# Alternating the two column halves of TensorE's array in a two-layer hybrid trunk

## The chip, the cores and the metric

The kernel runs on one core of a Trainium2 chip. The metric is device time in microseconds: the median of repeated executions, which agree with each other to a few hundredths of a per cent. Beside it stands one execution recorded by the hardware profiler, and all rows below come from that one.

The engines are called by their names in the profile: PE is TensorE's matmul side, PEld its weight loads, DVE is VectorE, ACT is ScalarE, POOL is GpSimd, SP the engine that issues the weight DMAs.

## The reference, cut to what matters

Two layers, 512 tokens, 1024 channels. Three mixers run side by side on one normalised input `h`, each is gated, projected and merged, and the result goes through an output projection onto the residual. Two of the mixers hold the products that the change touches:

```
# stick-breaking attention, 8 heads of 64 channels, 128-query blocks
z = q[:, start:end] @ k[:, :end].T * scale
w = where(causal, exp(log_sigmoid(z) + after), 0)      # after: sums of log_sigmoid(-z)
out = w @ v[:, :end]                                   # 64 channels per head

# state space, 32 groups of 16 channels, 64 complex states per group
h = associative_scan(a_bar, u @ b_bar)
y = h_re @ c_re - h_im @ c_im + d * u
```

Everything is in float32. The big projections are made of float32 values split into a high and a low part (three products each); the products of this change take plain float32 operands.

## The kernel before

**Slots.** A layer is a list of main products (`mm`, 24 or 12 passes over the array each), written out by hand in `ORDER_TEXT`. One main product is a slot. The mixers are Python generators beside it: a generator is spawned for a slot, issues some instructions, and says how many slots later it goes on. Its TensorE instructions stand before the main product of the slot (`advance`). The order on every engine is therefore fixed when the program is built; nothing is chosen at run time.

**Weights.** SP loads each weight tile (`raw`), ACT copies it into a high part (`wh`, L316), DVE subtracts to get the low part (`wl`, through the helper at L197). Four units are made ahead.

**Line numbers.** Every product and many vector operations go through counting helpers, so that their line is L197. They are told apart by the tile that they write.

**The attention output** (`sb_pair`, L1010, product `sbo`, L1097). A generator treats two heads. Each head has 64 channels, so its output has 64 rows: the first head's output goes to partitions 0 to 63 of one PSUM tile, the second head's to 64 to 127. Per head there are four products, one for each block of 128 keys, over 512, 384, 256 and 128 query columns, summed in PSUM. `v` is the stationary operand, [128 keys, 64 channels], so that a product occupies 64 of the array's 128 columns. There are four such generators in a layer, so eight `sbo` stretches in all. The transposed weights `wt0`, `wt13`, `wt2` come from `turned` (L1067), written by ACT and DVE a slot earlier.

**The state space output** (`ssm`, L870, product `py`, L917). A generator treats eight groups, in pairs of products: inputs times `mt` (the part within a chunk of tokens), then states `H` times `ca`, summed in PSUM. The stationary operand is [128, 64], the moving one 128 columns. Groups 0 to 3 go to partitions 0 to 63, groups 4 to 7 to 64 to 127. There are four such generators in a layer, so eight `py` stretches.

**Passes.** The trace shows each of these float32 products as two passes, each a weight load and a matmul record: 128 records stand for 64 products.

**The products of `within`** (tile `pk`, L773) are not touched. Each writes 32 partitions, so that it occupies a quarter of the array's columns, and the eight of them are issued to the four quarters in turn.

Of the kernel before, what the change touches and what calls it, by code (L numbers as in the profile page):

```python
# [27 lines left out]
# the products of a layer, in order: name, or name:first-last unit  # L28
# [6 lines left out]
# the schedule  # L35
K = dict(
    # tiles of the pools, and how far weights are loaded and split ahead
    nw=12, w=4, raw=4, b=48,
    # starts and distances of the parts beside the main products, in slots
    sb0=0, sb_gap=4, ssm0=6, ssm_gap=3, ret0=9, ret_gap=3, x0=-3, x1=2, ret_pre=4, lead=9,  # L40
    # shares of a slot that GpSimd and VectorE give to the tables
    g=0.9, v=0.7,
    # slots between the steps of a part
# [6 lines left out]
# columns of the combined input projection  # L50
# [8 lines left out]
# the products of a layer, in order: 512 columns by blocks of tokens ...  # L59
BY_TOKEN = "sq sk sv cu rq rk rv0 rv1 out0 out1".split()  # L60
# ... or one unit of weights at a time (eight products of 128 columns, or four of twice that)
# [7 lines left out]
# small parameters of a layer: columns of one [128, NPAR] array  # L69
# [16 lines left out]
def _tm(w, c0):  # L86
    """512 columns, four units of two 128-row blocks."""
    a = w[:, c0 : c0 + 512].reshape(4, 2, P, 512)
    return a.transpose(0, 2, 1, 3).reshape(4, P, 1024)


def _cm(w, c0):
    """128 columns, eight 128-row blocks: one unit."""
    return w[:, c0 : c0 + 128].reshape(8, P, 128).transpose(1, 0, 2).reshape(1, P, 1024)


def _cm2(w, c0):
    """256 columns of a matrix of 512 rows: one unit."""
    return w[:, c0 : c0 + 256].reshape(4, P, 2, 128).transpose(1, 2, 0, 3).reshape(1, P, 1024)


def _layout(i):
# [27 lines left out]
    for l in range(L):  # L130
        def put(n, a):
            c, s = PAR[n]
            par[l, :, c : c + s] = a

        def pg(a):  # [32, 64, ...] -> [(2 p), 32 ...]
            a = np.swapaxes(a, 0, 1).reshape(64, -1)
            return np.concatenate([a, a])

        put("rqg", i["ret_q_norm"][l][None])
        put("rkg", i["ret_k_norm"][l][None])  # L140
        put("sqg", np.tile(i["sb_q_norm"][l], 2)[:, None])
        put("skg", np.tile(i["sb_k_norm"][l], 2)[:, None])
        put("rog", i["ret_out_norm"][l].reshape(8, P).T)
        put("bglu", i["ssm_b_glu"][l].reshape(4, P).T)
        put("are", pg(i["ssm_a_re"][l]))
        put("aim", pg(i["ssm_a_im"][l]))
        put("ldt", pg(np.repeat(i["ssm_log_dt"][l][:, None], 64, 1)))
        # [(group of four, 2, channel), (quarter, half)]
        d = i["ssm_d"][l].reshape(4, 2, 4, 1, 16)
        put("dsk", np.broadcast_to(d, (4, 2, 4, 2, 16)).transpose(2, 3, 4, 0, 1).reshape(P, 8))  # L150
        for n in range(2):
            bc[l, n] = pg(i[("ssm_b_re", "ssm_b_im")[n]][l])
            bc[l, 2 + n] = pg(np.swapaxes(i[("ssm_c_re", "ssm_c_im")[n]][l], 1, 2))
# [4 lines left out]
def _constants():  # L158
    """Of shapes alone: rotary angles, retention's decays, masks."""
# [27 lines left out]
def trunk(ctx: ExitStack, tc, x_in, w_in, par_in, bc_in, ng_in, cst_in, rope_in, out):  # L187
# [3 lines left out]
    def counted(f, engine, each):  # L191
        """f, with its time in microseconds added to the load of its engine in this slot."""
# [63 lines left out]
    def spawn(gen, slot, front=False):  # L256
        """Start `gen` in a slot, one per main product. It yields how many slots later to go on: its products come
        before the slot's main one, 0 is for what follows them in the same slot."""
# [10 lines left out]
    def then(gen):  # L269
        """What follows a main product, in the next slot."""  # L270
        spawn(gen, now[0] + 1, True)

    def rsqrt_mean(out_, ssum, n, eps, cols):
        """out = (ssum / n + eps) ** -0.5 on Pool."""
# [18 lines left out]
    class Weights:  # L293
# [4 lines left out]
        def room(self, n):  # L298
            """Is there room for n more tiles: two of a unit in use, one of a loaded one?"""
# [36 lines left out]
    def three(ps, a, b, first, last):  # L336
        """ps += a.T @ b in float32's accuracy; a, b: (high, low) parts."""
# [13 lines left out]
    def token_major(lhs, evac):  # L351
        """512 columns of h @ w: one main product for each block of tokens."""
# [27 lines left out]
    def channel_piece(evac, rhs, nk, n, pair=None):  # L380
        """128 columns; with nk = 4 a unit holds two such."""
# [96 lines left out]
    # Its coefficients, of both layers at once  # L478
# [10 lines left out]
    def ks(n):  # L489
        """A temporary of the tables."""  # L490
# [13 lines left out]
    # powers e = 0 .. 8 of the discrete pole a: (Re, -Im) a^e above and (Im, Re) a^e below  # L504
    Y = [kc(n, NS * 9).rearrange("p (g e) -> p g e", e=9) for n in ("y_re", "y_im")]
    # unit phasors u = exp(8 i theta), conjugate above: fine[b] = u^(b+1), coarse[a] = u^(8 a)
# [3 lines left out]
    def cmul(o_re, o_im, a_re, a_im, b_re, b_im, tmp, eng=None):  # L510
        """o = a * b; tmp: three tiles' views like o."""
# [9 lines left out]
    def tables():  # L521
# [20 lines left out]
        # th: the angle in [-pi, pi]; sine and cosine from those of its half  # L542
# [17 lines left out]
        # q1: the discrete pole's conjugate  # L560
# [3 lines left out]
        # coef = (a_bar - 1) / a  # L564
# [35 lines left out]
        def times(tab, lo, m, to, a):  # L600
            """tab[to + i] = tab[lo + i] * a for i < m"""
# [26 lines left out]
        for m in (1, 2, 4):  # L628
            # coarse[m + 1 ...] = coarse[1 ...] * coarse[m]
# [10 lines left out]
    def cmul_steps(o_re, o_im, a_re, a_im, b_re, b_im, tmp, e=GT, every=1):  # L640
        """The same, an operation at a time."""
# [10 lines left out]
    class Coef:  # L652
        """One layer's matrices, emitted piece by piece."""
# [12 lines left out]
        def emit(self):  # L666
# [16 lines left out]
            # c's output is a real part: c below with the other sign  # L683
# [6 lines left out]
        def quarter(self, q, bb, cc):  # L690
# [19 lines left out]
            # states' input: a^(7-j) b  # L710
# [20 lines left out]
            # rotations exp(8 i theta (c + 1)), conjugate above  # L731
# [13 lines left out]
            # states' output: Re above, -Im below of c a^e, e = 0 .. 8  # L745
# [13 lines left out]
            # b for the products with it, twice  # L759
# [10 lines left out]
            # inputs within a chunk of eight tokens: Re(c a^(j-i) b), and the skip on the diagonal; two tokens' rows  # L770
            # at a time, the odd ones' a token later
# [36 lines left out]
    def layer(l, last, base):  # L808
# [23 lines left out]
        def qk_evac(dst, gain, l1, l2):  # L832
            """Normalised, transposed: [2 heads' channels, pair of heads, token]."""
# [36 lines left out]
        def ssm(q):  # L870
            win, ca, mt, T = coef.q[q]
            p0 = G * l + 8 * q
            # inputs of the groups, (token in chunk, channel) on partitions
# [14 lines left out]
            # rotate back, scan with the real decay, rotate on: the part by the sine comes from the other half  # L888
# [21 lines left out]
            # states after each chunk, moved on by one  # L910
# [5 lines left out]
            # the first four groups' chunks on the upper partitions, the others' on the lower  # L916
            py = psm("py")  # L917
            for n in range(8):
                sl = slice(n * 64, n * 64 + 64)
                o = py[64 * (n // 4) : 64 * (n // 4) + 64, n % 4 * P : n % 4 * P + P]  # L920
                k = 2 * (n % 2) + n // 4
                MM(o, ut[:, sl], mt[n % 4 // 2][:, k * P : k * P + P], start=True, stop=False)
                MM(o, H[:, sl], ca[:, n, 1:9, :].rearrange("p a b -> p (a b)"), start=False, stop=True)
# [15 lines left out]
            # gelu (tanh form): y * sigmoid(2 sqrt(2 / pi) (y + 0.044715 y^3))  # L939
# [68 lines left out]
        sbo = [None] * 4  # L1008

        def sb_pair(pr):  # L1010
# [3 lines left out]
            # by head: q's high part twice, and k's high and low parts, on the two halves of the partitions  # L1014
# [23 lines left out]
            def weights_of(ps, segs, sg):  # L1038
                """Stick-breaking weights, in sg; the running products of what is kept go from the right."""
# [58 lines left out]
            for h in range(2):  # L1098
                r = half[h]
                c = slice(128 * pr + 64 * h, 128 * pr + 64 * h + 64)  # L1100
                MM(po[r, :], sv[0][:, c], wt0[h], start=True, stop=False)
                MM(po[r, 128:512], sv[1][:, c], wt13[h][:, 0:384], start=False, stop=False)
                MM(po[r, 256:512], sv[2][:, c], wt2[:, 256 * h : 256 * h + 256], start=False, stop=False)
                MM(po[r, 384:512], sv[3][:, c], wt13[h][:, 384:512], start=False, stop=True)
# [15 lines left out]
        def load_rope(gain, rope):  # L1120
            # the norm's gain goes into the rotation's cosines and sines
# [48 lines left out]
        def ret_chunk(n):  # L1170
# [9 lines left out]
            def halves(c):  # L1180
                """By half: the parts of v, and the two parts of the others in one tile."""
# [131 lines left out]
        def quarters():  # L1313
            """The state space's quarters, as their matrices come."""
# [73 lines left out]
```

## Time and profile before

| what | value |
|---|---|
| median of 3 runs | 1353.73 us (1353.4 to 1353.94) |
| span of the profiled execution, first to last instruction | 1352.2 us |
| PE busy | 1321.8 us (98%) |
| PEld busy | 1069.4 us (79%) |
| DVE busy | 853.7 us (63%) |
| ACT, POOL busy | 537.0 us, 375.5 us |
| mean granted TensorE clock | 0.994 |

The profiled execution's own span is 1.5 us shorter than the median of the runs, which also holds what lies around the span. "Busy" of PE is the time in which at least one pass is somewhere in the array, and a pass stays in the records for longer than the distance to the next one, so that the share says nothing about how well the array's columns are filled. How long a stretch of products takes is read from the start of its first pass to the start of the first pass behind it.

In a timeline row, the first number is the start, the second the time that the merged group covers, "x16" the number of records merged, "128*64" the stationary operand's rows and columns, "128x512" the moving operand. In brackets stands the idle time of the engine before it and what ended it.

### The profile page before, as it was taken

The numbers are of one execution on the slowest core, as the hardware profiler recorded it, in microseconds if no ns is written. First come the engines' busy times: TensorE is split into PE (matmuls) and PEld (weight loads), VectorE is DVE, ScalarE is ACT, GpSimd is POOL, SyncE is SP. The second block draws the span as 40 slices with busy tenths as digits, with TensorE's granted clock in tenths as the row PEclk, the third lists the DMA queues.
The fourth block names the chain that finished last, engine by engine and source line by source line (L and its number), as shares of the span: only waits on it lengthen the run. The fifth ranks groups of instructions, "written<-read, shape, count | busy, mean of one in ns | idle before, by whom it ended". The sixth has DMA issues, their size and how long they took to land. (4 is left out here: it accounts for less than half of the span.)

```text
span 1352.2 us, 16611 instructions
## 1 busy us (share of the span) xinstructions
PE 1321.8 (98%) x6360; PEld 1069.4 (79%) x6360; DVE 853.7 (63%) x1189; ACT 537.0 (40%) x919; POOL 375.5 (28%) x436
## 2 busy tenths in 40 slices
PE   7989989999999999999999999899999999999998
PEld 5867768788887888888888777688888878888887
DVE  5996676776687338556365566778646845485542
ACT  5435433534434434332233444343443434333321
POOL 3230035737534013000052000576374420220000
PEclk9989989999999999999999999999999999999999
DMA  5332120222232221224533222112232224223332
GB/s 216 99 120 63 63 63 23 87 78 95 79 94 78 92 80 63 81 91 141 166 119 119 78 63 63 47 63 79 78 112 76 63 63 125 63 78 91 97 126 77
DMA packets 37375, 120.05 MB, mean 89 GB/s; under 512 B 4144, under 2 KB 4528, under 8 KB 37296
## 3 DMA queue, kind: packets, MB, share of 16 engines
q1 hardware_dynamic: 29664, 105.40, 24.6%
q10 hardware_dynamic: 7632, 13.59, 3.0%
q8 instruction: 50, 0.82, 0.2%
q14 instruction: 29, 0.24, 0.1%
HBM read 114.78 MB, written 4.19 MB: 88 GB/s over the span
## 5 line engine op out<-in xcount | busy, mean ns | idle before, releaser
L197 DVE TENSOR_TENSOR wl<-raw,wh 128x1024 fp32r<-128x1024 f32 x196 | 250.3, 1286 | 127.5 <-ACT wh L316 125.4
L197 PE MATMUL mm<-hh,wh 128*128 128x512 f32 x640 | 257.7, 403 | 0.0
L197 PE MATMUL mm<-hh,wl 128*128 128x512 f32 x640 | 253.1, 395 | 2.3 <-DVE wl L197 2.3
L197 PE MATMUL mm<-hl,wh 128*128 128x512 f32 x640 | 251.0, 392 | 0.0
L316 ACT ACTIVATE wh<-raw 128x1024 fp32r<-128x1024 f32 x196 | 206.0, 1057 | 85.7 <-PE mm L197 41.3
L197 PE MATMUL mm<-wh,hh 128*128 128x512 f32 x512 | 209.9, 410 | 0.8 <-ACT hh L419 0.8
L197 PE MATMUL mm<-wl,hh 128*128 128x512 f32 x512 | 204.9, 400 | 4.1 <-DVE wl L197 4.0
L197 PE MATMUL mm<-wh,hl 128*128 128x512 f32 x512 | 204.0, 399 | 0.0
L197 PEld LDWEIGHTS mm<-hh,wl 128*128 128x128 f32 x640 | 120.9, 189 | 30.6 <-DVE wl L197 3.6
L197 PEld LDWEIGHTS mm<-hh,wh 128*128 128x128 f32 x640 | 121.3, 190 | 24.8 <-issue 1.8
L197 PEld LDWEIGHTS mm<-hl,wh 128*128 128x128 f32 x640 | 121.2, 189 | 24.5
L197 PEld LDWEIGHTS mm<-wl,hh 128*128 128x128 f32 x512 | 104.9, 205 | 25.3 <-DVE wl L197 6.8
L197 PEld LDWEIGHTS mm<-wh,hh 128*128 128x128 f32 x512 | 104.7, 205 | 20.9 <-ACT hh L419 1.2
L197 PEld LDWEIGHTS mm<-wh,hl 128*128 128x128 f32 x512 | 104.6, 204 | 20.7 <-DVE hl L197 0.3
L1046 DVE TENSOR_TENSOR_SCAN kp<-kp,zero 128x511 f32<-128x511 f32 (+1 forms) x64 | 60.4, 964 | 36.8 <-ACT kp L1042 36.4
L987 ACT ACTIVATE gate<-mm 128x512 f32<-128x512 f32 x48 | 28.6, 595 | 123.4 <-PE mm L197 123.4
L197 POOL TENSOR_SCALAR ms<-ss 128x8 f32<-128x8 f32 (+3 forms) x56 | 19.1, 341 | 186.5 <-DVE ss L822 101.8
L1024 POOL CAST qd<-qd 64x512 fp32r<-64x512 f32 x16 | 15.8, 987 | 194.6 <-ACT qd L1020 179.6
L197 POOL TENSOR_TENSOR rs<-ms,mhalf 128x8 f32<-128x8 f32 (+3 forms) x56 | 64.7, 1155 | 4.7
L820 ACT ACTIVATE sq<-mm 128x512 f32<-128x512 f32 x32 | 19.0, 592 | 88.5 <-PE mm L197 88.5
L197 PE MATMUL mm<-wl,mgh 128*128 128x512 f32 x128 | 50.1, 391 | 0.2
L197 PE MATMUL mm<-wh,mgh 128*128 128x512 f32 x128 | 49.9, 390 | 0.0
(254 smaller groups left out, 2312.9 us busy)
## 6 DMA issues: line engine op xcount, KB each, us to landing
raw<-in_w SPq DMA_DIRECT2D x196, 512.0 KB, 3.5
x<-in_x SPq DMA_DIRECT2D x8, 256.0 KB, 7.3
rope<-in_rope ACTq DMA_DIRECT2D x8, 256.0 KB, 4.1
xh<-in_x ACTq DMA_DIRECT2D x8, 256.0 KB, 4.1
x<-xh ACTq DMA_DIRECT2D x8, 256.0 KB, 2.0
xh<-x ACTq DMA_DIRECT2D x8, 256.0 KB, 4.4
out<-xh ACTq DMA_DIRECT2D x8, 256.0 KB, 2.0
gB<-in_ng SPq DMA_DIRECT2D x2, 256.0 KB, 6.0
```

Source lines behind the costliest of these rows:

```text
L197: return f(*a, **k)
L316: ACT(wh, raw, AF.Copy)
L820: ACT(s2, ps, AF.Square)
L987: ACT(sg, ps, AF.Sigmoid)
L1024: nc.gpsimd.tensor_copy(out=qd[h][o, :], in_=qd[h][r, :])
L1046: nc.vector.tensor_tensor_scan(v, v, zero1.to_broadcast([P, n - 1]), 1.0, ALU.mult, ALU.add)
```

## The change

The products are the same, with the same operands and the same sums. Only the order in which they are issued changes. In `sbo`, the loop over heads is now inside the loop over key blocks. In `py`, group `i` of the first four and group `i + 4` are issued in turn, first both products with `mt`, then both with `ca`. All comments and docstrings are also gone, which moves line numbers.

```diff
             py = psm("py")
-            for n in range(8):
-                sl = slice(n * 64, n * 64 + 64)
-                o = py[64 * (n // 4) : 64 * (n // 4) + 64, n % 4 * P : n % 4 * P + P]
-                k = 2 * (n % 2) + n // 4
-                MM(o, ut[:, sl], mt[n % 4 // 2][:, k * P : k * P + P], start=True, stop=False)
-                MM(o, H[:, sl], ca[:, n, 1:9, :].rearrange("p a b -> p (a b)"), start=False, stop=True)
+            for i in range(4):
+
+                for part in range(2):
+                    for n in (i, i + 4):
+                        sl = slice(n * 64, n * 64 + 64)
+                        o = py[64 * (n // 4) : 64 * (n // 4) + 64, n % 4 * P : n % 4 * P + P]
+                        k = 2 * (n % 2) + n // 4
+                        if part == 0:
+                            MM(o, ut[:, sl], mt[n % 4 // 2][:, k * P : k * P + P], start=True, stop=False)
+                        else:
+                            MM(o, H[:, sl], ca[:, n, 1:9, :].rearrange("p a b -> p (a b)"), start=False, stop=True)
...
             po = psm("sbo")
-            for h in range(2):
-                r = half[h]
-                c = slice(128 * pr + 64 * h, 128 * pr + 64 * h + 64)
-                MM(po[r, :], sv[0][:, c], wt0[h], start=True, stop=False)
-                MM(po[r, 128:512], sv[1][:, c], wt13[h][:, 0:384], start=False, stop=False)
-                MM(po[r, 256:512], sv[2][:, c], wt2[:, 256 * h : 256 * h + 256], start=False, stop=False)
-                MM(po[r, 384:512], sv[3][:, c], wt13[h][:, 384:512], start=False, stop=True)
+            for kb in range(4):
+
+                for h in range(2):
+                    c = slice(128 * pr + 64 * h, 128 * pr + 64 * h + 64)
+                    w = (wt0[h], wt13[h][:, 0:384], wt2[:, 256 * h : 256 * h + 256], wt13[h][:, 384:512])[kb]
+                    MM(po[half[h], 128 * kb : 512], sv[kb][:, c], w, start=kb == 0, stop=kb == 3)
```

On PE, the first `sbo` stretch of the first layer stands so before (`wt_1159`, `wt_1160` are the first head's `wt0` and `wt13`, `wt_1293`, `wt_1294` the second head's, and `wt_1012` is `wt2` with both heads in it; "waits" names the engines whose semaphores the row waits for):

```order
L197 MATMUL sbo<-wt_1159,sv 64x512 [waits Activation_49]
L197 MATMUL sbo<-wt_1160,sv 64x384
L197 MATMUL sbo<-wt_1012,sv 64x256
L197 MATMUL sbo<-wt_1160,sv 64x128
L197 MATMUL sbo<-wt_1293,sv 64x512
L197 MATMUL sbo<-wt_1294,sv 64x384 [waits DVE_49]
L197 MATMUL sbo<-wt_1012,sv 64x256 [waits Activation_49]
L197 MATMUL sbo<-wt_1294,sv 64x128
L197 MATMUL mm<-hh,wh 128x512
```

and so with the change:

```order
L197 MATMUL sbo<-wt_1159,sv 64x512 [waits Activation_49]
L197 MATMUL sbo<-wt_1293,sv 64x512
L197 MATMUL sbo<-wt_1160,sv 64x384
L197 MATMUL sbo<-wt_1294,sv 64x384 [waits DVE_49]
L197 MATMUL sbo<-wt_1012,sv 64x256
L197 MATMUL sbo<-wt_1012,sv 64x256 [waits Activation_49]
L197 MATMUL sbo<-wt_1160,sv 64x128
L197 MATMUL sbo<-wt_1294,sv 64x128
L197 MATMUL mm<-hh,wh 128x512
```

The second head's products have moved up between the first head's; the wait for DVE stands at the fourth product instead of the sixth. The first `py` stretch on PE stands so with the change, where "x2" is one product for each half in turn (before, `mt` and `ca` alternate in eight such pairs, the four pairs of the lower half first):

```order
L197 MATMUL py<-mt_2000,ut 64x128 [waits PE_49]
L197 MATMUL py<-mt_2000,ut 64x128
L197 MATMUL py<-ca,H 64x128 [waits DVE_49,Pool_49]
L197 MATMUL py<-ca,H 64x128
L197 MATMUL py<-mt_2000,ut 64x128 x2
L197 MATMUL py<-ca,H 64x128 x2
L197 MATMUL py<-mt_2001,ut 64x128 x2
L197 MATMUL py<-ca,H 64x128 x2
L197 MATMUL py<-mt_2001,ut 64x128 x2
L197 MATMUL py<-ca,H 64x128 x2
L197 MATMUL mm<-hh,wh 128x512
```

The order of instructions on DVE, ACT, POOL and SP is the same as before.

## Rows read from the trace of the kernel before

**Rows 1.** The page: span, then busy time, share, instructions; clock by slices.

```profile
span 1352.2 us, 16611 instructions
...
PE 1321.8 (98%) x6360; PEld 1069.4 (79%) x6360; DVE 853.7 (63%) x1189; ACT 537.0 (40%) x919; POOL 375.5 (28%) x436
...
PEclk9989989999999999999999999999999999999999
```

**Rows 2.** Waits of PE: waited for, us in total, times, longest.

```profile
PE T L396 <- DVE xn L197: 8.7, 2, 7.9
PE wt L1063 <- DVE w L197: 8.1, 4, 2.4
PE mm L197 <- DVE wl L197: 6.3, 7, 1.5
```

**Rows 3.** Timeline of PE and PEld, first and last sbo stretch.

```profile
133.44 3.93 PE L197 MATMUL sbo<-wt,sv 128*64 128x512 f32 x16
...
133.44 0.19 PEld L197 LDWEIGHTS sbo<-wt,sv 128*64 128x64 f32 x2
133.92 0.14 PEld L197 LDWEIGHTS sbo<-wt,sv 128*64 128x64 f32 x1 [0.29 <-issue]
134.35 0.14 PEld L197 LDWEIGHTS sbo<-wt,sv 128*64 128x64 f32 x1 [0.29 <-issue]
134.67 0.14 PEld L197 LDWEIGHTS sbo<-wt,sv 128*64 128x64 f32 x1 [0.18 <-issue]
135.00 0.62 PEld L197 LDWEIGHTS sbo<-wt,sv 128*64 128x64 f32 x6 [0.19 <-issue]
135.91 0.14 PEld L197 LDWEIGHTS sbo<-wt,sv 128*64 128x64 f32 x1 [0.29 <-issue]
...
137.30 0.50 PE L197 MATMUL mm<-hh,wh 128*128 128x512 f32 x1
...
906.02 3.93 PE L197 MATMUL sbo<-wt,sv 128*64 128x512 f32 x16
909.88 0.50 PE L197 MATMUL mm<-hh,wh 128*128 128x512 f32 x1
```

**Rows 4.** Timeline of PE in windows at 135.30 and 135.50: passes then running.

```profile
134.99 0.65 PE L197 MATMUL sbo<-wt,sv 128*64 128x256 f32 x3
...
135.00 1.07 PE L197 MATMUL sbo<-wt,sv 128*64 128x512 f32 x4
```

**Rows 5.** Timeline of PE, first py stretch cut, and the last one's ends.

```profile
285.91 0.43 PE L197 MATMUL py<-mt,ut 128*64 128x128 f32 x2
286.18 0.38 PE L197 MATMUL py<-ca,H 128*64 128x128 f32 x2
286.40 0.38 PE L197 MATMUL py<-mt,ut 128*64 128x128 f32 x2
...
287.27 0.44 PE L197 MATMUL py<-mt,ut 128*64 128x128 f32 x4
287.49 0.44 PE L197 MATMUL py<-ca,H 128*64 128x128 f32 x4
287.76 0.38 PE L197 MATMUL py<-mt,ut 128*64 128x128 f32 x2
...
289.17 0.51 PE L197 MATMUL mm<-hh,wh 128*128 128x512 f32 x1
...
1063.33 0.43 PE L197 MATMUL py<-mt,ut 128*64 128x128 f32 x2
...
1066.59 0.33 PE L396 MATMUL T<-ident,m 128*128 128x128 f32 x1
```

**Rows 6.** Timeline of PE and PEld around one pk stretch.

```profile
264.19 0.64 PE L197 MATMUL pk<-ca,b 128*32 128x128 f32 x16
264.77 0.66 PE L396 MATMUL T<-ident,U 128*128 128x128 f32 x4
...
264.19 0.38 PEld L197 LDWEIGHTS pk<-ca,b 128*32 128x32 f32 x16 [0.35 <-issue]
```

**Rows 7.** Timeline rows before three waits of PE, by engine.

```profile
184.50 0.60 ACT L987 ACTIVATE gate<-mm 128x512 f32<-128x512 f32 x1 [3.64 <-PE mm L197]
...
185.65 0.68 DVE L197 TENSOR_TENSOR ql<-sqk,qd 64x512 fp32r<-64x512 f32 x1 [3.08 <-ACT qd L1020]
...
197.21 2.18 PE L1063 MATMUL wt<-ident,w 128*128 128x128 f32 x9 [2.41 <-DVE w L197]
...
228.18 0.60 ACT L1042 ACTIVATE kp<-z 128x512 f32<-128x512 f32 x1 [0.50 <-PE z L197]
...
228.81 2.54 DVE L1046 TENSOR_TENSOR_SCAN kp<-kp,zero 128x127 f32<-128x127 f32 x2 [3.37 <-ACT kp L1042]
...
237.52 0.50 PE L197 MATMUL mm<-hh,wl 128*128 128x512 f32 x1 [0.63 <-DVE wl L197]
...
422.15 0.60 ACT L1163 ACTIVATE rv<-mm 128x512 f32<-128x512 f32 x1 [4.43 <-PE mm L197]
...
430.28 0.50 PE L197 MATMUL mm<-wl,hh 128*128 128x512 f32 x1 [1.46 <-DVE wl L197]
```

**Rows 8.** Timeline: DVE copies at the fourth and third sbo; fourth sbo on PE.

```profile
241.37 0.68 DVE L1070 COPY wt<-wt 128x512 f32<-128x512 f32 x1
...
212.13 0.69 DVE L1107 COPY sbo<-sbo 128x512 f32<-128x512 f32 x1
...
242.77 3.93 PE L197 MATMUL sbo<-wt,sv 128*64 128x512 f32 x16
```

**Rows 9.** Stretches: us, PE, PEld, DVE, ACT, POOL busy (records), PEclk, DMA, GB/s.

```profile
195.00:202.00 7.00, 4.79 (x16) 4.24 (x17) 6.70 (x7) 0.98 (x2) 3.40 (x4) 0.51 0.17 44
...
860.50:864.00 3.50, 2.69 (x11) 2.62 (x12) 3.41 (x4) 0.98 (x2) 2.08 (x3) 0.52 0.00 0
```

## The prediction

> **What bounds the kernel now.** I read the page first: PE is busy for 1321.8 of 1352.2 us, the next engine, DVE, for 853.7 [rows 1]. The waits of PE come next: the three largest kinds add to 23.1 us [rows 2]. So TensorE's stream of passes sets the time, and a microsecond less of it is a microsecond less of the span wherever no other engine sets the pace for it. The share does not say how well the array is filled, so I then read the two kinds of stretch that the change touches, pass by pass, in the timeline.
>
> A `sbo` stretch lasts from 133.44 to the next main product at 137.30: 3.86 us. The last of the eight is as long, 906.02 to 909.88 [rows 3]. A `py` stretch lasts from 285.91 to 289.17, 3.26 us, and the last one from 1063.33 to 1066.59 as well [rows 5]. Eight of each make 8 x (3.86 + 3.26) = 57.0 us, in which each pass uses half of the array's columns. That bounds the matter: if the halves could do everything side by side, about half of 57 us would go.
>
> **Do two halves run side by side here?** The trace of before already has short stretches of it, where the program turns from one half to the other.
>
> In `sbo` the first head's weight loads start at 133.44 (two of them), 133.92, 134.35 and 134.67, and then six come within 0.62 us, from 135.00 on [rows 3]. At 135.50 four passes run, the oldest of them of 512 columns and begun at 135.00 [rows 4]. The first head's own 512-column passes began at 133.44 and 133.92, so this is the second head's, and the first head had then loaded only five or six of its eight stationary operands. At 135.30 it runs with two passes of 256 columns, which are the first head's [rows 4]. So the second head's work started ahead of some of the first head's and ran beside it.
>
> At what pace? From its first load to its third, the first head takes 133.44 to 134.35 = 0.91 us; the second head, sharing the array, 135.00 to 135.91 = 0.91 us [rows 3]. Sharing cost nothing. In `py` a pair of passes comes every 0.22 us where one half works (286.18, 286.40); at the turn four come with start at 287.27 and four at 287.49, still 0.22 us apart, so twice as many [rows 5].
>
> The longest proof is `pk`: products on quarters of the columns, issued to the four in turn, sixteen passes, and the next product starts 264.77 - 264.19 = 0.58 us after the first [rows 6]. One after another at 0.11 us each they would need 1.76. So alternating order gives side-by-side work, and the front end delivered sixteen loads within 0.38 us [rows 6]. With two halves of 64 columns, `py` asks for one load per 0.055 us, which is less than that.
>
> **The change, part by part.** No product is added or removed, and no other engine's order moves. What changes is the order inside sixteen stretches.
>
> *`sbo`.* With the change, both heads run through their eight passes together. One head alone, the second one, takes 135.00 to 137.30 = 2.30 us, start to next main product, and it was slowed by nothing [rows 3]. The other head starts about one load later; I add 0.05. So 2.35 instead of 3.86: 1.51 saved, and 1.56 at the best (2.30).
>
> *`py`.* The second half's sixteen passes start at 287.27 (with the four of `py<-mt`) and the next main product at 289.17: 1.90 us [rows 5]. With the same 0.05 the stretch takes 1.95 instead of 3.26: 1.31 saved, 1.36 at the best.
>
> *The waits in the stretch.* In `sbo`, the wait for DVE's copy `wt13` of the second head stands two products earlier, and so does the use of `wt0`. Where this is tightest, in the fourth pair, that copy ends at 241.37 + 0.68 = 242.05 [rows 8]; the stretch begins at 242.77 there, 0.72 later [rows 8], so the wait is already over. This costs nothing. It would cost what the copy is late if DVE's queue were 0.7 us longer ahead of it.
>
> *Sum.* 8 x (1.51 + 1.31) = 22.6 us. In the profiled execution's time that is 1352.2 - 22.6 = 1329.6 for the span, and with the 1.5 us by which the median of the runs exceeds it, 1353.7 - 22.6 = **1331.1 us**. The best values of both give 8 x 2.92 = 23.4, so 1330.4.
>
> **Where the saving could be lost.** A shorter stretch brings PE earlier to whatever it waits for. The saving survives if that wait hangs on PE itself. I followed the waits in layer 0 (layer 1 repeats them). The wait for `w` that ends at 197.21 goes back along DVE to 185.65, where DVE had idled 3.08 us for ACT, and ACT had idled until 184.50 for a main product of PE [rows 7]. The wait for `wl` that ends at 237.52 goes back to DVE at 228.81, which had idled 3.37 us for ACT's `kp`, which waited for PE's `z` [rows 7]. The wait that ends at 430.28 goes back to ACT at 422.15, idle 4.43 us for PE [rows 7]. In all three, PE starts the chain, so the chain moves forward with it, and the idle ahead of it (3.08, 3.37, 4.43) is more than the 1.5 us that one stretch gives. The place with the least room is the third `sbo`: DVE copies it out at 212.13, with no idle time ahead of the copy, so it comes directly from other work and does not get there earlier [rows 8]. The next chain behind it is the one with 3.37 us idle, which covers 1.51. Without that cover, 1.5 us would return in each layer.
>
> **One cost I can only bound.** Behind the same wait for `w`, the granted clock falls to its lower level (1.2 instead of 2.4 GHz): for 7.0 us at 0.51 in layer 0, and only for 3.5 us at 0.52 in layer 1 [rows 9]. The two places have the same products, so the length depends on something that the order of work does not show. With all times shifted, either may go to the other's length: 3.5 us at half clock is 1.7 us of work, so -1.7 in layer 0, +1.7 in layer 1. I take zero and keep both ends.
>
> **Rivals.**
>
> *Starts in program order.* Suppose a pass could start only when the one before it in the program has started. Then two passes of one product, which share a half, hold up the next product: the second head's first pass starts with the first head's second pass, and the next product of the first head waits until the second head's second pass starts. I follow this through with passes of 0.43, 0.32, 0.21 and 0.11 us for 512, 384, 256 and 128 columns (the first two are distances of loads in [rows 3], the last is half of 0.22 in [rows 5], the third is twice that, rounded). One head alone starts its last pass after 2 x 0.43 + 2 x 0.32 + 2 x 0.21 + 0.11 = 2.03 us, so 0.27 of its 2.30 is the start and the end. In program order the last pass of both starts after one 0.43 more, 2.46; with 0.27 that is 2.73, 1.13 saved. `py` takes 16 x 0.11 for its starts instead of 15 x 0.11 in 1.90, so 2.01, 1.25 saved. Sum 8 x 2.38 = 19.0, so 1334.7. Against it: the pass that began at 135.00 ahead of passes that the program has before it [rows 3, 4]. For it: nothing in the trace, but I saw only overtaking over a few passes. 1 in 10.
> The Trainium skill states this order as a rule: "TensorE: Matmul & The Clock Gate", in Part 3 on packing small matmuls, says that matmuls are monotone in program order in start and in end, without reordering. The trace disagrees where it can be seen, as just told; by the page's rule the time would be the 1334.7 of this rival, by the rows the 1331.1 above.
>
> *The saving is partly given back.* DVE is the engine that PE waits for. If the third `sbo` of each layer and one more stretch before each wait bring nothing, 4 x 1.5 = 6 us are lost: 1337. For it: DVE is busy nearly throughout around those places. Against it: the idle times above. 1 in 10.
>
> *The turn is not free, and the halves do not share.* If two halves ran one after the other, the overlap that before has would go too: two heads at 2.30 less one end of 0.2 are 4.40, 0.54 more than now; `py` 2 x 1.90 - 0.2 = 3.60, 0.34 more; 8 x 0.88 = 7, so 1361, slower. If each of the 20 added turns per pair of stretches also emptied the array as the last turn to full width does (0.2 us from pass to pass instead of 0.11), 8 x 20 x 0.09 = 14 more: 1375. It decides as soon as alternation stops the sharing. Against it: `pk`, which alternates [rows 6]. 4 in 100.
>
> *Nothing changes*, because TensorE reorders deep enough already: then the turn in `sbo` would not show only four or so passes of overlap. 2 in 100, 1353.7.
>
> **How the numbers follow.** The first case has 74 in 100, around 1331.1. Its own range is 1327 to 1335: 23.4 us saved and 3.4 gained by the clock at both places gives 1326.9; 22.6 saved less 3.4 lost gives 1334.5. The program-order case ends at 1334.7, 1338 with a lost clock stretch, and most of the given-back case lies below 1338. So 1327 to 1338 leaves out the 6 in 100 of the last two rivals and some of the others. Faster by over 0.2% (2.7 us, about what a measurement of this kernel can tell from none) 0.94, same 0.02, slower 0.04.
>
> **What the profile after would show.** Right: `sbo` stretches of about 2.35 us and `py` of about 1.95, the same number of passes, the three waits of PE as long as now. Program order: 2.7 and 2.0. Given back: PE waits for `wl` or `w` that sum to more than the 14.4 of now [rows 2]. The prediction is wrong if the stretches are not shorter than 2.7 and 2.1, or if the waits eat more than 5 us.

## The result, and the profile after

The changed kernel takes 1330.49 us (median of 4 runs, 1329.82 to 1332.1) against 1353.84 us for the kernel before, timed beside it. The ratio is 0.9826, with a 95% interval of 0.9813 to 0.984: 23.35 us faster. The forecast was 22.6 us less, 1331.1 us.

The page of the changed kernel, the same lines as in [rows 1]:

```profile
span 1330.4 us, 16615 instructions
PE 1299.4 (98%) x6360; PEld 1051.4 (79%) x6360; DVE 854.5 (64%) x1189; ACT 537.7 (40%) x919; POOL 371.3 (28%) x436
```

The number of passes is the same, 6360. PE is still busy 98% of a span that is 21.8 us shorter: the busy share did not move at all, and says nothing of what happened. DVE and ACT have the same work. The profiled execution took 1332.1 us, the longest of the four runs, so it shows 21.8 instead of 23.35.

The timeline of PE and PEld of the changed kernel in the first `sbo` stretch, then PE alone in the last one:

```profile
132.97 2.38 PE L197 MATMUL sbo<-wt,sv 128*64 128x512 f32 x16
135.28 0.50 PE L197 MATMUL mm<-hh,wh 128*128 128x512 f32 x1
...
132.97 0.20 PEld L197 LDWEIGHTS sbo<-wt,sv 128*64 128x64 f32 x4
133.46 0.14 PEld L197 LDWEIGHTS sbo<-wt,sv 128*64 128x64 f32 x2 [0.29 <-issue]
133.89 0.14 PEld L197 LDWEIGHTS sbo<-wt,sv 128*64 128x64 f32 x2 [0.29 <-issue]
...
890.95 2.37 PE L197 MATMUL sbo<-wt,sv 128*64 128x512 f32 x16
893.25 0.51 PE L197 MATMUL mm<-hh,wh 128*128 128x512 f32 x1
```

The stretch lasts 135.28 - 132.97 = 2.31 us, and the last 893.25 - 890.95 = 2.30, instead of 3.86 [rows 3]. The loads stand where the first head's stood before, at 0.49 and 0.92 us from the start (before, 0.48 and 0.91), but two at a time. Four loads, both heads' first two, take 0.20 us, about as long as two took before (0.19).

The timeline of PE in the first `py` stretch, shortened:

```profile
280.07 0.44 PE L197 MATMUL py<-mt,ut 128*64 128x128 f32 x4
280.34 0.39 PE L197 MATMUL py<-ca,H 128*64 128x128 f32 x4
280.56 0.39 PE L197 MATMUL py<-mt,ut 128*64 128x128 f32 x4
...
281.97 0.51 PE L197 MATMUL mm<-hh,wh 128*128 128x512 f32 x1
```

Every 0.22 us four passes start instead of two, and the stretch takes 1.90 us instead of 3.26 [rows 5]. All eight stretches of each kind have these lengths within 0.01 us. So the gain by the rows is 8 x (3.86 - 2.30) + 8 x (3.26 - 1.90) = 12.5 + 10.9 = 23.4 us, which is the measured 23.35. That they agree to a tenth is partly luck: the four runs lie 2.3 us apart, and this execution's span shows only 21.8, since places outside the sixteen stretches took 1.6 us more in it than in the profiled execution of before.

The waits of PE, as in [rows 2]:

```profile
PE T L396 <- DVE xn L197: 8.9, 2, 7.3
PE wt L1068 <- DVE w L197: 8.1, 4, 2.4
PE mm L197 <- DVE wl L197: 6.3, 7, 1.5
```

The waits for `w` and `wl` are what they were, to the tenth of a microsecond and in number. Nothing was given back there.

A little was given back at a place that this view does not show, where the projection takes up the fourth pair's result, whose low part is `ybl`. The timelines of PE and PEld with the change, then of PE before, at the same passes:

```profile
254.62 0.39 PE L197 MATMUL mm<-ybh,wh 128*128 128x512 f32 x1
254.83 0.19 PEld L197 LDWEIGHTS mm<-ybl,wh 128*128 128x128 f32 x1 [0.24 <-DVE ybl L197]
255.77 0.40 PE L197 MATMUL mm<-ybl,wh 128*128 128x512 f32 x1
...
260.70 0.39 PE L197 MATMUL mm<-ybh,wh 128*128 128x512 f32 x1
261.61 0.39 PE L197 MATMUL mm<-ybl,wh 128*128 128x512 f32 x1
```

The weight load of `ybl` now has to wait for DVE, and the four passes from the first of these rows to the last take 1.15 us instead of 0.91. The same happens in layer 1, so 0.5 us in all. It is small, but this place has no room left.

### The profile page after: what moved, and what is told of

Its sections match the earlier page's. It is cut to its first block, busy times and chain, and to the rows that moved or that the text cites. A ratio compares the mean times of both kernels' runs of the same rounds, so it can differ in the third digit from the quotient of the medians.

```text
span 1330.4 us, 16615 instructions
## 1 busy us (share of the span) xinstructions
PE 1299.4 (98%) x6360; PEld 1051.4 (79%) x6360; DVE 854.5 (64%) x1189; ACT 537.7 (40%) x919; POOL 371.3 (28%) x436
```

## The experiments

**One part at a time.** The first kernel keeps the old order in `py`, the second in `sbo`:

```diff
 # attention only
-            for i in range(4):
-                for part in range(2):
-                    for n in (i, i + 4):
+            for n in range(8):
...
 # state space only
-            for kb in range(4):
-                for h in range(2):
+            for h in range(2):
...
```

> Only the attention output alternates; the state space output stands as before. Theory (two halves of the columns run side by side at full pace, whatever the program order): the sbo stretch takes 2.30 us, the py stretch 3.26, and 8 x (3.86 - 2.30) = 12.4 us go, so about 1341.3 us. Rival (a part of the gain came from somewhere else, such as later stretches or the clock): the time differs from that by more than 2 us, or this and the state space alone do not add up to the 23.4 us of both.

> Only the state space output alternates; the attention output stands as before. Theory: py takes 1.90 us, sbo 3.86, and 8 x (3.26 - 1.90) = 10.9 us go, so about 1342.9 us. Rival: as for the attention alone; more than 2 us away, or no sum with it.

Attention alone: 1341.41 us, ratio 0.9909 (0.9895 to 0.9922), 12.5 us less than the 1353.88 beside it. State space alone: 1343.51 us, ratio 0.9922 (0.991 to 0.9935), 10.4 us less. The stretches in the timeline of PE, first the `sbo` and `py` ends of attention alone, then of state space alone:

```profile
132.24 2.37 PE L197 MATMUL sbo<-wt,sv 128*64 128x512 f32 x16
134.54 0.50 PE L197 MATMUL mm<-hh,wh 128*128 128x512 f32 x1
...
277.92 0.43 PE L197 MATMUL py<-mt,ut 128*64 128x128 f32 x2
...
281.18 0.51 PE L197 MATMUL mm<-hh,wh 128*128 128x512 f32 x1
```

```profile
132.87 3.93 PE L197 MATMUL sbo<-wt,sv 128*64 128x512 f32 x16
136.73 0.50 PE L197 MATMUL mm<-hh,wh 128*128 128x512 f32 x1
...
285.09 0.44 PE L197 MATMUL py<-mt,ut 128*64 128x128 f32 x4
...
286.98 0.51 PE L197 MATMUL mm<-hh,wh 128*128 128x512 f32 x1
```

Each part shortens its own stretch (2.30 and 1.89) and leaves the other as it was (3.86 and 3.26). 12.5 + 10.4 = 22.9 against 23.35 for both: the parts add up within the spread of the runs, which is some 2.3 us in each of the three changed kernels.

**The same order on one half of the columns.** The second head's and the second groups' outputs go to partitions 0 to 63 of a second tile:

```diff
-                        o = py[64 * (n // 4) : 64 * (n // 4) + 64, n % 4 * P : n % 4 * P + P]
+                        o = (py, py2)[n // 4][0:64, n % 4 * P : n % 4 * P + P]
...
-                    MM(po[half[h], 128 * kb : 512], sv[kb][:, c], w, start=kb == 0, stop=kb == 3)
+                    MM(po[h][0:64, 128 * kb : 512], sv[kb][:, c], w, start=kb == 0, stop=kb == 3)
```

> The order of the change, but the outputs of both streams go to partitions 0 to 63, of two PSUM tiles, so that all products use the same half of the array's columns; the evacuations are split in two. Theory (the half of the array decides, not the order): sixteen passes one after the other, so sbo takes 2 x 2.03 + 0.27 = 4.33 us and py 32 x 0.11 + 0.2 = 3.7 us, some 0.45 us more than before in each, and the whole about 8 x 0.9 = 7 us more than before, 1361, with 1 to 3 us more for the second evacuations. Rival (alternating hides something between two products of one sum, such as a wait of a product for the sum before it or for its weight load): sbo and py are nearer to 2.30 and 1.90 than to 4.33 and 3.7.

It took 1361.16 us in its one run. The timeline of PE, first stretch of each:

```profile
132.53 4.52 PE L197 MATMUL sbo<-wt,sv 128*64 128x512 f32 x16
136.98 0.50 PE L197 MATMUL mm<-hh,wh 128*128 128x512 f32 x1
...
286.55 0.65 PE L197 MATMUL py<-mt,ut 128*64 128x128 f32 x4
287.04 0.60 PE L197 MATMUL py<-ca,H 128*64 128x128 f32 x4
287.48 0.60 PE L197 MATMUL py<-mt,ut 128*64 128x128 f32 x4
...
290.19 0.51 PE L197 MATMUL mm<-hh,wh 128*128 128x512 f32 x1
```

`sbo` takes 4.45 us and `py` 3.64, where 4.33 and 3.7 were expected: the same products in the same alternating order, but four passes of `py` now need 0.44 us instead of 0.22. So alternating by itself hides nothing; the gain is that the two streams lie on different columns (and so on different partitions of the output). It is also longer than before by 0.59 and 0.38 us, which is the overlap at the one turn that the old order had. 8 x 0.97 = 7.8 us more than before, and 1353.9 + 7.8 = 1361.7. For the second evacuations 1 to 3 us more were expected; in this one run nothing of it shows.

**Two at a time.** How fine must the alternation be? Here two products of a half stand together:

```diff
             for i in range(4):
-                for part in range(2):
-                    for n in (i, i + 4):
+                for n in (i, i + 4):
+                    for part in range(2):
...
-            for kb in range(4):
-                for h in range(2):
+            for kbs in (0, 1), (2, 3):
+                for h in range(2):
+                    for kb in kbs:
```

> As the change, but two products of one half stand together before the other half's two: in sbo the key blocks 0 and 1 of the first head, then of the second, then 2 and 3; in py both products of group i, then both of group i + 4. Theory (TensorE looks four passes, two products, ahead of the running one, as the overlap of before shows): nothing is lost, sbo 2.30 us and py 1.90, the time as with the change, 1330.5. Rival (turns must follow pass by pass, or starts go in program order): sbo about 3.0 and py about 2.1 us, so some 7 us more, 1338.

1330.53 us (1330.36 to 1332.05), ratio 0.9831 (0.9815 to 0.9846), the same as the change. The timeline of PE:

```profile
132.68 2.42 PE L197 MATMUL sbo<-wt,sv 128*64 128x512 f32 x16
135.04 0.50 PE L197 MATMUL mm<-hh,wh 128*128 128x512 f32 x1
...
278.80 0.45 PE L197 MATMUL py<-mt,ut 128*64 128x128 f32 x4
...
280.75 0.51 PE L197 MATMUL mm<-hh,wh 128*128 128x512 f32 x1
```

2.36 and 1.95 us: 0.05 more in each stretch, 0.8 us in all, less than the runs differ. The 3.0 and 2.1 us of the rival did not come. Four passes of one half ahead of the other's do not hold it up.

**Four at a time, and quarters by two.** In `py` eight passes of a half stand together; in `pk`, which the change left as it was, two products of a quarter do:

```diff
-            for i in range(4):
-                for part in range(2):
-                    for n in (i, i + 4):
+            for n in (0, 1, 4, 5, 2, 3, 6, 7):
...
+                    for part in range(2):
...
-                for g in range(8):
+                for g in (0, 4, 1, 5, 2, 6, 3, 7):
```

> The attention output as with the change. In the state space output four products (eight passes) of one half stand together, then four of the other, twice each. And the products of the untouched tile pk on quarters of the columns are issued two to a quarter at a time instead of one. Theory A (each group of columns has its own queue, which takes the running pass and three more; the program's order is held up only when the queue that is next is full): py takes 2.34 to 2.39 us (the second half starts 0.44 us late, the first half's second part waits for it), pk 0.58 to 0.65. Theory B (TensorE looks four passes ahead of the oldest running one over the whole program): py the same 2.3 to 2.4, but pk about 1.0 us, since only two quarters fit into the look ahead. Rival C (it looks ahead far, the earlier overlap of before was limited by something else): py stays at 1.90 to 1.95. Time by A 8 x 0.45 = 3.6 us more than the change, 1334; by B 1337.

1335.38 us in its one run. The timeline of PE, one `py` stretch shortened and one `pk` stretch, with the row of a window at 256.96, which shows what then runs:

```profile
278.61 0.43 PE L197 MATMUL py<-mt,ut 128*64 128x128 f32 x2
...
279.10 0.44 PE L197 MATMUL py<-mt,ut 128*64 128x128 f32 x4
...
280.58 0.38 PE L197 MATMUL py<-mt,ut 128*64 128x128 f32 x2
...
281.11 0.51 PE L197 MATMUL mm<-hh,wh 128*128 128x512 f32 x1
...
256.92 0.67 PE L197 MATMUL pk<-ca,b 128*32 128x128 f32 x16
...
256.92 0.34 PE L197 MATMUL pk<-ca,b 128*32 128x128 f32 x4
...
257.52 0.55 PE L396 MATMUL T<-ident,U 128*128 128x128 f32 x3
```

Now the first four passes run alone (rows of x2), the other half joins 0.49 us after the start, when three of the eight passes ahead of it have still to start after the running one, and the last four run alone again: 2.50 us. Before, the other half joined with three passes left as well (1.36 us after the start, behind twelve of sixteen passes [rows 5]). The 2.50 us are longer than the change (1.90) and shorter than one turn (3.26). `pk` takes 0.60 us instead of 0.58 [rows 6], not 1.0, and 0.04 us after its start four passes run. Passes on the same columns follow each other by 0.11 us, so it is one in each quarter, although the last of them has twelve passes ahead of it in the program. Of the three theories only A fits: each group of columns takes its running pass and three more out of the program's order, whatever the other groups do. If TensorE looked only four passes ahead over the whole program, two quarters could have run at a time. The size of `py` was 0.11 to 0.16 us off, which fits the start of a new stream (the first pass of one takes 0.05 longer) counted too few times. Time: 8 x 0.60 + 8 x 0.02 = 5.0 more than the change, 1335.5.

**A slot more for the transposes.** The one expectation that failed clearly:

```diff
-                yield K["b3"]
+                yield K["b3"] + (h == 0)
```

> The change, and the first head's softer deadline: the step that transposes its weights comes one slot (one main product, 5.5 us) later. The prediction rests on the claim that PE's wait for w hangs on a chain that PE itself starts. By that theory a slot of room covers the wait (2 x 4.6 us between three passes, of which some 0.3 are work), so about 8.6 us go, and 3 to 6 us more if the lower clock behind these waits goes too: 1316 to 1322. Rival (DVE is short of time in that stretch as a whole): the wait comes back at another place, as a wait for wl or at the transposes of the second head, and the time is within 3 us of the change's 1330.5.

1336.17 us, ratio 0.9874 (0.9857 to 0.989): 5.7 us slower than the change, where 8 to 14 less were expected. The waits of PE, and two rows of the timeline of PE:

```profile
PE wt L1068 <- DVE w L197: 4.1, 6, 0.8
...
PE mm L197 <- ACT ybh L282: 2.4, 2, 1.2
PE mm L197 <- DVE ybl L197: 1.8, 2, 0.9
...
253.58 0.50 PE L197 MATMUL mm<-ybh,wh 128*128 128x512 f32 x1 [1.24 <-ACT ybh L282]
254.95 0.69 PE L197 MATMUL mm<-ybl,wh 128*128 128x512 f32 x1 [0.87 <-DVE ybl L197]
```

The wait for `w` went from 8.1 to 4.1 us, so room does shrink it. But every later step of a pair moves by a slot with it, up to the last pair's result, which had no room left with the change, and now the projection waits for it: `ybh` and `ybl`, 4.2 us that were not there. The rival was right in kind (the wait comes back elsewhere) and too mild in size.

All waits in this view add to 26.3 us, against 26.9 with the change, so they are not what is longer. By an estimate, the clock is most of it. Main products alone, summed over the stretches at the lower level, with the change and then in this kernel:

```profile
sum 17.07, PE 9.84 PEld 8.01 DVE 0.00 ACT 0.58; mean PE 3.28 PEld 2.67 DVE 0.00 ACT 0.19
...
sum 20.46, PE 18.64 PEld 14.41 DVE 2.23 ACT 0.58; mean PE 3.73 PEld 2.88 DVE 0.45 ACT 0.12
```

There are five such stretches instead of three. Two are new, 3.4 us each; they begin directly behind the new waits (at 255.09 and 910.45 us) and are full of main products. So main products are busy at half the clock for 18.64 us instead of 9.84. If half of the 8.8 us more is lost, that is 4.4 us (the estimate), beside the 4.2 by which the two profiled executions differ (1334.6 and 1330.4). The rest of the 5.7 us between the medians comes from the change's profiled execution being the longest of its four. What each small wait adds to this is left open. No version faster than the change came out of this.

## Why the prediction was right, point by point

**The halves run side by side at full pace.** Shown by the change and by the same order on one half. The proof that the prediction took from `pk` and from the turn inside the old stretches held.

**The sizes.** `sbo` was put at 2.35 us and measured 2.30, `py` at 1.95 and 1.90. The 0.05 us that I added for the second stream's later start is not there: two streams that alternate start together, and the best values (23.4 us, 1330.4) were the true ones. 16 x 0.05 = 0.8 us is the difference between the forecast 22.6 and 23.4.

**The wait for the second head's copy.** Nothing, as said: all eight `sbo` stretches have the same length, the tight fourth one too. One reading was off without harm: the use of the second head's `wt0` stands three products earlier, not two.

**What hangs on PE.** The idle time of DVE ahead of the wait for `wl` was 3.37 us [rows 7]. After the change, the timeline of DVE there, with the third and the fourth copy of `sbo`:

```profile
224.28 2.54 DVE L1051 TENSOR_TENSOR_SCAN kp<-kp,zero 128x127 f32<-128x127 f32 x2 [2.02 <-ACT kp L1047]
...
209.73 0.68 DVE L1111 COPY sbo<-sbo 128x512 f32<-128x512 f32 x1
240.69 0.69 DVE L1111 COPY sbo<-sbo 128x512 f32<-128x512 f32 x1 [0.96 <-PE sbo L197]
```

The idle time gave 3.37 - 2.02 = 1.35 us, and the third copy still comes directly behind DVE's own work, as [rows 8] showed. This is the cover that the prediction named, and some 2 us of it are left. A second saving of this kind ahead of the same place would use most of it.

**The clock.** The prediction put it at zero with 3.4 us to either side. The stretches at the lower level (1.2 GHz), in the view by stretches of the changed kernel, and last the one at 93 us before:

```profile
192.80:199.70 6.90, 6.06 (x19) 5.22 (x20) 5.66 (x6) 0.98 (x2) 2.11 (x3) 0.51 0.27 76
844.80:851.60 6.80, 4.64 (x16) 4.09 (x17) 6.50 (x7) 0.98 (x2) 3.35 (x4) 0.50 0.17 30
93.80:97.30 3.50, 2.84 (x7) 2.27 (x8) 3.41 (x4) 2.77 (x4) 0.00 (x0) 0.51 0.00 0
...
92.60:99.50 6.90, 6.00 (x14) 4.74 (x15) 5.72 (x6) 4.97 (x6) 0.00 (x0) 0.51 0.18 58
```

The one in layer 1 grew from 3.5 [rows 9] to 6.8 us, as it might; a third one, at 93 us, which the prediction did not look at, shrank from 6.9 to 3.5. In the sum nothing, so that zero came out; that one grew as the other shrank is luck. What a stretch costs was put too high: PE is busy for 4.64 of the 6.8 us in layer 1, against 2.69 of 3.5 [rows 9], so 1.95 us more of work ran at half the clock, which costs about 1.0 us (an estimate) and not the 1.7 that the prediction took, since part of the stretch is spent waiting. The spread of the four runs goes with it: the two at a mean granted clock of 0.994 took 1329.82 and 1329.87 us, the two at 0.993 took 1331.12 and 1332.1.

**The rivals.** Starts in program order would have given 2.73 and 2.01 us; measured are 2.30 and 1.90, and both passes of the second head's first product are loaded in the same 0.20 us as the first head's, ahead of where that order allows them. The rule of the Trainium skill ("TensorE: Matmul & The Clock Gate", Part 3 on packing small matmuls) that matmuls start in program order does not hold for the two halves here. Given back were 0.5 us at `ybl`, not the 6 of that rival and not where it looked, and alternating did not end the sharing.

## What to carry to other kernels

Where products use half (or a quarter) of the array's columns and their outputs go to different partitions, issue the halves in turn: with the float32 products of this kernel the passes then run side by side at full pace, and the time of the stretch is that of one half. It need not be pass by pass; up to four passes of one half may stand together, while with eight the stretch was a third longer (2.50 us against 1.90). A busy share of 98% does not tell that half of the array stands empty: look at the stationary operand's shape in the timeline, and at stretches where the program turns from one half to the other, which show the gain before it is made. And look at what is due behind a stretch that becomes shorter: here one such place, `ybl`, lost all its room, and a later step by one slot cost 5.7 us.

## What was not expected of the hardware

A second stream of passes on the other half starts practically with the first: four weight loads of 64 columns covered 0.20 us, two covered 0.19. And the look ahead is counted per group of columns, about four passes in each, since all four quarters ran 0.04 us after the start with four passes of each standing together (0.60 us against 0.58), while with eight passes of a half together the other half joined only 0.49 us after the start.
